# A hybrid encoder layer on one core: side tasks cut into steps at each change of engine, and residual pieces emitted one a k tile

## The chip, the cores and the metric

The kernel runs on one NeuronCore of a Trainium2 chip. The metric is the device time of one execution in microseconds (us); lower is better. The core has a matrix engine (PE, with its weight loads shown apart as PEld), three engines for everything else (DVE, ACT and POOL), and a queue for transfers (SP). Each engine works through its own instructions strictly in the order in which the program emitted them, and waits on semaphores for what others produce.

## What is computed

One layer of an encoder on 256 tokens of width 2048, in float32:

```
h = rmsnorm(x);  q,k,v (8 heads x 128), u (512), q_mem (4 heads x 128) = h @ w_in
y_na  = neighbourhood attention over the 256 tokens, learned bias per head
y_ssm = S5 state space mixer: increments, a scan in both directions, output, GELU, GLU
y_mem = cross attention of q_mem into 256 memory tokens (w_mem_kv)
x = x + rmsnorm(concat(rmsnorm(y_na), rmsnorm(y_ssm), rmsnorm(y_mem)) @ w_out)
x = x + rmsnorm(square(relu(rmsnorm(x) @ w_ff1)) @ w_ff2)
```

## The kernel before

All weights come as one stream of chunks of 128 x 1024 floats, in the order in which PE uses them. Each chunk is loaded (`wraw`, three buffers), rounded on ACT to a high part (`wh`) and subtracted on DVE to a low part (`wl`), so that each product of float32 is made of three (in the MLP of two wider) PE products. `take()` hands the next tile of weights to the main stream, and at each new chunk first emits the conversion of the chunk two ahead. So a conversion that stands late in ACT's or DVE's queue holds up PE two chunks later.

Between the main products stand side tasks, written as Python generators: attention heads (`att_task`: scores, softmax `P`, transposes `PT`, output), preparation of the state space matrices (`prep_b`, `prep_c`, `k0`), its increments (`incr`), its scan (`tree`, products `ps` and sums `XS` on DVE alone), its output (`ssm_out`), and the splits of results into high and low parts. `tick()`, called twice a chunk, lets tasks take steps up to their next `yield`. Nothing of this runs on the chip: it fixes the order in which each engine's instructions are emitted.

The order is set by a planner. It keeps a clock for each engine (`clk["V"]` for DVE, `"A"` for ACT, `"G"` for POOL, `"E"` for PE), and every instruction books a cost on its engine's clock (a DVE product of n elements, for one, 72 + 1.04 n ns). Within one step `chain` carries the end of one engine's work into the start of the next one's; a new step starts with an empty chain. After a plain `yield` the task's next step may be taken when PE's clock has passed the chain's end plus `MARGIN` (200 ns), for attention tasks 1200 ns more; after `yield True` it may be taken at once, as long as the engine's clock is not ahead of PE's by more than a bound (2600 ns on DVE, 3000 on ACT, 1700 for the scan). A plain `yield` behind a series of `yield True` has booked nothing in its own step, so the step behind it may be taken at the next tick.

The second edit stands at the head of the MLP. There the residual x1 = x + normed output of the mixer is made in column pieces (`x1_part`): ACT (for the last 512 columns DVE) scales the piece of `acc1`, POOL adds it to `x1`, each twice, once for 128 tokens. `h_prep(k)` transposes columns 128 k on of `x1` on PE and splits them into `hs`. The first MLP product runs over k tiles of 128 rows, with six outputs each, and emits `h_prep(k + 2)` ahead of tile k. Columns 0 to 512 are made ahead of the loop, the rest in six pieces of 256 columns inside it; piece j is transposed first by the `h_prep` that stands ahead of k tile 2 j + 2.

Of the kernel before, what the change touches and what calls it, by code (L numbers as in the profile page):

```python
# [102 lines left out]
def hybrid_kernel(ctx: ExitStack, tc: tile.TileContext, A: dict, out: bass.AP, dbg=None):  # L103
# [81 lines left out]
    def act(o, i, f=AF.Copy, **kw):  # L185
        ACT.activation(o, i, f, **kw)

    def split(h, l, src, g):

        act(h, src, AF.Copy, scale=g)  # L190
        stt(l, src, g, h.bitcast(F32), mult, sub)
# [79 lines left out]

    def wait_for(g):
        while live(g):
            yield


# [379 lines left out]
    def prep_b(ut):  # L656
        yield from until(lambda: ut in loaded and clk["E"] > loaded[ut][1])
        raw = loaded[ut][0]
        w = a2.tile([128, 2, 2, 4, 4, 16], F32, name="W", tag="W", bufs=1)
        par = a2.tile([128, 4, 2, 2, 4], F32, name="par", tag="par", bufs=1)  # L660
        for i, x in enumerate((cfr, cfi, lbr, lbi)):
            act(par[:, i], x[:, 8 * ut:8 * ut + 8].rearrange("p (d q) -> p d q", d=2)[:, :, None, :]
                .to_broadcast([128, 2, 2, 4]))
        for l in range(4):
            o = w[:, :, :, :, l, :]
            src = (w[:, :, :, :, l - 1, :].rearrange("p d c q b -> p (d c q) b") if l
                   else raw.rearrange("p (n b) -> p n b", b=16))
            r_, i_ = (par[:, 2 * min(l, 1) + i].rearrange("p d c q -> p (d c q)")[:, :, None].to_broadcast([128, 16, 16])
                      for i in range(2))
            t = a2.tile([128, 2, 2, 4, 16], F32, name="pt", tag="pt", bufs=1)  # L670
            tt(V, t.rearrange("p d c q b -> p (d c q) b"), src, i_, mult)
            tt(V, o.rearrange("p d c q b -> p (d c q) b"), src, r_, mult)
            tt(V, o[:, :, 0], o[:, :, 0], t[:, :, 1], sub)
            tt(V, o[:, :, 1], o[:, :, 1], t[:, :, 0], add)
            yield True
        yield
        act(W0[ut].rearrange("p d c q j b -> p (d c q) j b"),
            w[:, :, :, :, 0, :].rearrange("p d c q b -> p (d c q) b")[:, :, None, :].to_broadcast([128, 16, 2, 16]))
        w0_done.add(ut)
        if ut % 2 == 0:  # L680
            XS[ut // 2] = a2.tile([128, 2, 16, NB], F32, name="XS", tag="AB", bufs=2)
        for d in range(2):
            for j in range(2):
                h = slice(64 * j, 64 * j + 64)
                act(wx[h, :, ::-1 if d == 0 else 1, j, :], w[h, d].rearrange("p c q l b -> p (c q) l b"))
            yield
            wt = a2.tile([128, 2, 4, 128], F32, name="W1T", tag="W1T", bufs=2)
            for c in range(2):
                p = att()
                for q in range(4):  # L690
                    PE.transpose(p[:, q * 128:(q + 1) * 128], wx[:, 4 * c + q].rearrange("p l j b -> p (l j b)"), ident)
                act(wt[:, c].rearrange("p q m -> p (q m)"), p)
            spawn(incr(ut, d, wt, clk["A"] + MARGIN), 2, "A")
            yield
        yield from until(lambda: (ut, 1) in xs_part)
# [20 lines left out]
    def prep_c(ut):  # L716
        cw = a2.tile([128, 4, 2, 8, 16], F32, name="Cw", tag="ps" if ut < 2 else "W", bufs=1)
        nc.sync.dma_start(cw[:, 0], A["c"][:, ut])
        yield from after(6000.0)
        act(cw[:, 0, 1], cw[:, 0, 1], AF.Copy, scale=-1.0)  # L720
        for l in range(1, 4):
            C, L = cw[:, l - 1], cw[:, l]
            t = a2.tile([128, 2, 8, 16], F32, name="pt", tag="pt", bufs=1)
            tt(V, t, C, bcd(lbi, ut, 1, 16), mult)
            tt(V, L, C, bcd(lbr, ut, 1, 16), mult)
            tt(V, L[:, 0], L[:, 0], t[:, 1], add)
            tt(V, L[:, 1], L[:, 1], t[:, 0], sub)
            yield True
        yield
        for j in range(2):  # L730
            h = slice(64 * j, 64 * j + 64)
            act(CCs[ut % 2][h, :, 16 * j:16 * j + 16], cw[h].rearrange("p l c q b -> p (l c q) b"))
        CC[ut] = CCs[ut % 2].rearrange("p (l c q) b -> p l c q b", l=4, c=2)
        yield
# [21 lines left out]
    def tree(g):  # L756

        X = XS[g]
        cols = slice(16 * g, 16 * g + 16)
        for up, l in [(1, l) for l in range(LEV)] + [(0, l) for l in range(LEV - 2, -1, -1)]:  # L760
            h = 1 << l
            d0 = 2 * h - 1 if up else 3 * h - 1
            n = len(range(d0, NB, 2 * h))
            dst, src = X[:, :, :, d0::2 * h], X[:, :, :, d0 - h:NB - h:2 * h]
            t = a2.tile([128, 2, 16, NB // 2], F32, name="ps", tag="ps", bufs=1)[:, :, :, 0:n]
            tt(V, t, src[:, ::-1], pw[:, l, 0:2, cols][:, :, :, None].to_broadcast([128, 2, 16, n]), mult)
            yield True
            tt(V, dst, dst, t, add)
            yield True
            tt(V, t, src, pw[:, l, 2, cols][:, None, :, None].to_broadcast([128, 2, 16, n]), mult)  # L770
            yield True
            tt(V, dst, dst, t, add)
            yield True
        yield

    yg = uT
    yHL = {}
# [1 line left out]
    def ssm_out(ut):  # L779
        p = att()  # L780
        BD = BD2[:, ut % 2]
        for n, (m, i, k, o) in enumerate(((0, 0, 3, 0), (3, 1, 3, 1), (1, 0, 2, 1), (4, 2, 2, 1), (2, 0, 1, 2),
                                          (5, 3, 1, 1))):
            PE.matmul(p[:, o * NB:(o + k) * NB], BD[:, m, :], uT[:, ut, i * NB:(i + k) * NB], start=(n == 0),
                      stop=False, skip_group_check=True)
        H = XS[ut // 2]
        for i in range(4):
            for d in range(2):
                l = (i + 1) % 4 if d == 0 else (4 - i) % 4
                for c in range(2):  # L790
                    for q in range(4):
                        h = H[:, c, 8 * (ut % 2) + 4 * d + q, :]

                        if d == 0:
                            o0, h = (1, h[:, 0:NB - 1]) if l else (0, h)
                        else:
                            o0, h = (0, h[:, NB - 2::-1]) if l else (0, h[:, ::-1])
                        n = NB - 1 if l else NB
                        PE.matmul(p[32 * q:32 * q + 32, i * NB + o0:i * NB + o0 + n], CC[ut][:, l, c, 4 * d + q, :],
                                  h, start=False, stop=(i == 3 and d == 1 and c == 1), skip_group_check=True,  # L800
                                  tile_position=(0, 32 * q))

        y = yg[:, ut, :]
        t = a2.tile([128, 256], F32, name="gt", tag="gt", bufs=1)
        stt(y, y, col(V_D, ut), p[:, 0:256], mult, add)
        act(t, y, AF.Square)
        out_done.add(ut)
        yield
        ts(t, t, 0.044715, mult, 1.0, add, eng=G)
        tt(G, t, t, y, mult)  # L810
        act(t, t, AF.Tanh, scale=math.sqrt(2.0 / math.pi))
        yield
        stt(yg[:, ut, :], t, 1.0, y, add, mult)
        if dbg:
            dbg(f"y{ut}", y)
        yield
# [42 lines left out]
    def ssm_fin():  # L859
        yHL["H"] = a2.tile([128, 4, 256], F32R, name="yH", tag="AB", bufs=2)  # L860
        yHL["L"] = a2.tile([128, 4, 256], F32R, name="yL", tag="AB", bufs=2)
        half = const.tile([128, 1], F32, name="half")
        V.memset(half, 0.5)
        for ut in range(4):
            split(yHL["H"][:, ut, :], yHL["L"][:, ut, :], yg[:, ut, :], half)
            yield True


    def att_task(qk, vt, bias, hl, name, gcol):
# [15 lines left out]
            act(P[:, t, :], P[:, t, :], AF.Exp, bias=mn[:, t:t + 1], scale=-1.0, accum_out=sm[:, t:t + 1])  # L885
        yield
        V.reciprocal(sm, sm)
        for t in range(2):
            act(P[:, t, :], P[:, t, :], AF.Copy, scale=sm[:, t:t + 1])
        yield  # L890
# [12 lines left out]
        if gcol is None:  # L903
            act(hl, p[:, 0:256])
        else:
            split(hl[0], hl[1], p[:, 0:256], gcol)
        sumsq(name, p[:, 0:256])
        yield


    for ut in range(2):
# [142 lines left out]
    def na_fin():  # L1054
        for h in range(NAH):
            yield from wait_for(naT[h])
            split(mixn[:, 0, h, :], mixn[:, 1, h, :], yna[:, h, :], col(V_NA, h))
            yield

    def na_rms():  # L1060
        yield from wait_for(nf)
# [206 lines left out]
    for k in range(KT):  # L1268
# [12 lines left out]
                PE.matmul(pg[o][:, 256:512], w[1 - i], hs[:, k, i, :], start=False, stop=False, skip_group_check=True)  # L1281
        if k == 0:
            h_prep(2)
        if k % 2 == 0 and k < 12:
            x1_part(slice(128 * k + 512, 128 * k + 768))
    A1.close()
    C = ExitStack()
    cp = C.enter_context(tc.tile_pool(name="cp", bufs=1, side="left"))
# [203 lines left out]
```

## Time and profile before

| | |
|---|---|
| median of 3 runs | 1166.17 us (1164.01 to 1166.64) |
| the profiled execution | 1163.6 us, its span 1161.8 us, mean granted PE clock 0.992 |
| PE busy | 1127.8 us, 97% of the span |
| DVE, ACT, POOL busy | 718.3, 586.0, 94.7 us |
| HBM | 182 GB/s over the span |

The rows further down come from the profiled execution. Times in them are us from the start of the span; an engine's row has start, length, engine, line (L154 is the helper that records every operation, so rows are told apart by their tiles), operation, output <- inputs, and in brackets the idle time of the engine ahead of it with what ended it.

### The profile page before, as it was taken

Reading aid. Unit: us, or ns where it says so; the run is one execution under the profiler, and the core shown is the slowest. Engines: PE = TensorE matmul, PEld = TensorE weight load, DVE = VectorE, ACT = ScalarE, POOL = GpSimd, SP = SyncE. Lnnn points to the kernel's source line nnn. Section 1 sums busy time; section 2 is a strip of 40 time slices with the busy share of each in tenths; the row PEclk is TensorE's granted clock in tenths of the full one; section 3 lists DMA queues with packets and bytes.
Section 4 is the critical chain, followed back from the end, with each engine's and each line's share of the span. In section 5 each row is a group of like instructions: output and inputs, shape, how many; then the busy total and the mean of one; then the engine's idle time right before and its main releaser. Section 6 shows DMA issues by size and latency. Waiting matters only on the chain.

```text
span 1161.8 us, 17423 instructions
## 1 busy us (share of the span) xinstructions
PE 1127.8 (97%) x6776; PEld 972.8 (84%) x6776; DVE 718.3 (62%) x1066; ACT 586.0 (50%) x908; POOL 94.7 (8%) x163
## 2 busy tenths in 40 slices
PE   8999998899999998999999999999999999999996
PEld 8988898789878877888888888888888888888885
DVE  7778477887875675776665444445666665454454
ACT  6586755635663565554455434434444444344341
POOL 1850000000000043000000000000000000011000
PEclk9999999999999999999999999999999999999999
DMA  8874453344444675556666666566666666666663
GB/s 317 291 237 148 149 168 104 106 142 150 138 153 126 205 233 172 176 187 187 193 192 188 184 190 189 181 197 185 195 185 194 187 188 192 186 197 195 190 210 128
DMA packets 62723, 213.05 MB, mean 183 GB/s; under 512 B 7216, under 2 KB 8752, under 8 KB 62640
## 3 DMA queue, kind: packets, MB, share of 16 engines
q1 hardware_dynamic: 62352, 211.84, 58.1%
q8 instruction: 53, 0.87, 0.3%
q14 instruction: 30, 0.25, 0.1%
q10 hardware_dynamic: 288, 0.09, 0.0%
HBM read 209.81 MB, written 2.10 MB: 182 GB/s over the span
## 4 chain that ended last, share of the span: by engine, by line
PE 78%; DVE 6%; ACT 5%; POOL 4%; DMA 3%; issue 3%; SPq 0%; DVEq 0%; ACTq 0%; POOLq 0%
PE acc L154 70%; PE att L154 4%; DMA wraw<-in_w_dram 3%; PE big L154 3%; DVE wl L154 3%; ACT wh L154 3%; POOL x L154 1%; DVE XS L154 1%; ACT P L154 1%; POOL u L154 1%; DVE ps L154 1%; POOL acc L154 0%; ACT wx L154 0%; POOL t L154 0%; POOL q L154 0%
## 5 line engine op out<-in xcount | busy, mean ns | idle before, releaser
L154 DVE TENSOR_TENSOR wl<-wraw,wh 128x1024 fp32r<-128x1024 f32 (+1 forms) x372 | 455.3, 1226 | 383.8 <-ACT wh L154 383.2
L154 ACT ACTIVATE wh<-wraw 128x1024 fp32r<-128x1024 f32 (+1 forms) x372 | 391.2, 1053 | 418.4 <-PE acc L154 340.4
L154 PE MATMUL acc<-hs,wh 128*128 128x512 f32 (+1 forms) x996 | 345.9, 391 | 0.0
L154 PE MATMUL acc<-hs,wl 128*128 128x256 f32 x992 | 279.3, 282 | 0.0
L154 PEld LDWEIGHTS acc<-hs,wh 128*128 128x128 f32 x996 | 186.8, 188 | 38.8 <-ACT hs L154 0.2
L154 PEld LDWEIGHTS acc<-hs,wl 128*128 128x128 f32 x992 | 187.3, 189 | 0.0
L154 PE MATMUL acc<-wh,fH 128*128 128x512 f32 x448 | 178.7, 399 | 0.0
L154 PE MATMUL acc<-wh,fL 128*128 128x512 f32 x448 | 176.5, 394 | 0.0
L154 PE MATMUL acc<-wl,fH 128*128 128x512 f32 x448 | 175.7, 392 | 0.0
L154 PEld LDWEIGHTS acc<-wh,fL 128*128 128x128 f32 x448 | 84.1, 188 | 22.0
L154 PEld LDWEIGHTS acc<-wl,fH 128*128 128x128 f32 x448 | 84.1, 188 | 19.8
L154 PEld LDWEIGHTS acc<-wh,fH 128*128 128x128 f32 x448 | 84.1, 188 | 19.4
L154 PE MATMUL acc<-xH,wh 128*128 128x256 f32 x256 | 75.6, 295 | 0.0
L154 PE MATMUL acc<-xH,wl 128*128 128x256 f32 x256 | 72.4, 283 | 0.0
L154 PE MATMUL acc<-xL,wh 128*128 128x256 f32 x256 | 72.4, 283 | 0.0
L154 PEld LDWEIGHTS acc<-xH,wh 128*128 128x128 f32 x256 | 48.9, 191 | 0.8
L154 PEld LDWEIGHTS acc<-xL,wh 128*128 128x128 f32 x256 | 48.9, 191 | 0.4
L154 PEld LDWEIGHTS acc<-xH,wl 128*128 128x128 f32 x256 | 48.8, 191 | 0.0
L154 POOL TENSOR_TENSOR facc<-facc,g 128x512 f32<-128x512 f32 x6 | 9.0, 1528 | 475.1 <-DMA g<-in_g_dram 475.1
L154 PE MATMUL acc<-wh,mixn 128*128 128x512 f32 x128 | 42.1, 404 | 0.0
L154 DVE TENSOR_TENSOR ps<-XS,pw 128x32 f32<-128x32 f32 (+9 forms) x44 | 30.8, 700 | 1.1
L154 DVE TENSOR_TENSOR XS<-XS,ps 128x32 f32<-128x32 f32 (+9 forms) x44 | 29.4, 668 | 0.8
(304 smaller groups left out, 1486.2 us busy)
## 6 DMA issues: line engine op xcount, KB each, us to landing
wraw<-in_w_dram SPq DMA_DIRECT2D x369, 512.0 KB, 4.3
tokst<-in_xt_dram SPq DMA_DIRECT2D x4, 512.0 KB, 6.8
mst<-in_memT_dram SPq DMA_DIRECT2D x4, 512.0 KB, 5.1
tokst<-in_mt_dram SPq DMA_DIRECT2D x4, 512.0 KB, 5.8
bias<-in_bias_dram SPq DMA_DIRECT2D x8, 256.0 KB, 4.0
x<-in_xt_dram SPq DMA_DIRECT2D x8, 256.0 KB, 5.1
out_dram<-facc SPq DMA_DIRECT2D x8, 256.0 KB, 2.5
xst<-in_xT_dram SPq DMA_DIRECT2D x7, 256.0 KB, 5.8
```

Source lines behind the costliest of these rows:

```text
L154: return f(o, *a, **kw)
```

## The change

Two edits. The first: a step of a side task now ends where its work goes from one engine to another. Where there was a plain `yield` (or nothing) behind a series on ACT or DVE, `done(e)` lets the task go on only when PE's clock has passed that engine's booked end plus 200 ns. `split_task` puts a step's end between the high part on ACT and the low part on DVE; `att_task` gets one behind the reciprocal and one ahead of the low part of a memory head; `ssm_out` gets two. The second: the residual pieces are emitted behind k tiles 0 to 5 and not behind 0, 2, 4, ... 10. Instructions, sizes and buffers stay the same.

```diff
+    def split_task(h, l, src, g):
+        act(h, src, AF.Copy, scale=g)
+        yield
+        stt(l, src, g, h.bitcast(F32), mult, sub)
...
+    def done(e):
+
+        t = clk[e] + MARGIN
+        while clk["E"] < t:
             yield
...
@@ prep_b
                 .to_broadcast([128, 2, 2, 4]))
+        yield from done("A")
...
             yield True
-        yield
+        yield from done("V")
...
@@ prep_c
         act(cw[:, 0, 1], cw[:, 0, 1], AF.Copy, scale=-1.0)
+        yield from done("A")
...
             yield True
-        yield
+        yield from done("V")
...
@@ tree
             tt(V, dst, dst, t, add)
             yield True
-        yield
+        yield from done("V")
...
@@ ssm_out
         stt(y, y, col(V_D, ut), p[:, 0:256], mult, add)
+        out_done.add(ut)
+        yield
         act(t, y, AF.Square)
-        out_done.add(ut)
         yield
         ts(t, t, 0.044715, mult, 1.0, add, eng=G)
         tt(G, t, t, y, mult)
+        yield
         act(t, t, AF.Tanh, scale=math.sqrt(2.0 / math.pi))
...
@@ att_task
         V.reciprocal(sm, sm)
+        yield
         for t in range(2):
             act(P[:, t, :], P[:, t, :], AF.Copy, scale=sm[:, t:t + 1])
...
-            split(hl[0], hl[1], p[:, 0:256], gcol)
+            act(hl[0], p[:, 0:256], AF.Copy, scale=gcol)
         sumsq(name, p[:, 0:256])
         yield
+        if gcol is not None:
+            stt(hl[1], p[:, 0:256], gcol, hl[0].bitcast(F32), mult, sub)
+            yield
...
@@ na_fin
-            split(mixn[:, 0, h, :], mixn[:, 1, h, :], yna[:, h, :], col(V_NA, h))
-            yield
+            yield from split_task(mixn[:, 0, h, :], mixn[:, 1, h, :], yna[:, h, :], col(V_NA, h))
...
@@ the MLP's first product
-        if k % 2 == 0 and k < 12:
-            x1_part(slice(128 * k + 512, 128 * k + 768))
+        if k < 6:
+            x1_part(slice(256 * k + 512, 256 * k + 768))
```

What this does to the engines' orders shows at three places.

The end of the second scan on DVE, before. `ps` and `XS` of 32x31 are the scan's last level; `ssm_out` on PE, which reads `XS`, stands in PE's order among the products of the output projection (`mixn`), 12 main products behind the place where the projection's head results begin.

```order
L154 TENSOR_TENSOR wl<-wraw,wh 128x1024
L154 TENSOR_TENSOR ps<-XS,pw 128x32x31
L154 TENSOR_TENSOR XS<-XS,ps 128x32x31
L154 SCALAR_TENSOR_TENSOR mixn<-yna,vecs,mixn 128x256 x3
L154 TENSOR_TENSOR ps<-XS,pw 128x32x31
L154 SCALAR_TENSOR_TENSOR mixn<-yna,vecs,mixn 128x256
L154 TENSOR_TENSOR wl<-wraw,wh 128x1024
L154 TENSOR_TENSOR XS<-XS,ps 128x32x31
```

The same end in the changed kernel. It now stands ten conversions earlier, between those of the last head's weights (conversions are counted in DVE's order), and `ssm_out` stands among the products of the last head, 120 main products earlier in PE's order.

```order
L154 TENSOR_TENSOR wl<-wraw,wh 128x1024
L154 SCALAR_TENSOR_TENSOR P<-att,bias 128x512
L154 TENSOR_REDUCE mn<-P 128x2
L154 TENSOR_TENSOR XS<-XS,ps 128x32x31
L154 TENSOR_TENSOR wl<-wraw,wh 128x1024
L154 TENSOR_TENSOR ps<-XS,pw 128x32x31
L154 TENSOR_TENSOR XS<-XS,ps 128x32x31
```

The densest place of the changed kernel on ACT, in the stretch of the first four heads. `W1T` goes to an increment's products on PE, `PT` to a head's output, `wx` and `P` to transposes.

```order
L154 ACTIVATE wh<-wraw 128x1024
L154 ACTIVATE PT<-att 128x512
L154 ACTIVATE P<-P,sm 128x256 x2
L154 ACTIVATE XS<-att 128x2x256
L154 ACTIVATE wx<-W 64x32x16 x2
L154 ACTIVATE mixm<-att,vecs 128x256
L154 ACTIVATE sq<-att 128x256
L154 ACTIVATE PT<-att 128x512
L154 ACTIVATE P,sm<-P,mn 128x256 x2
L154 ACTIVATE W1T<-att 128x512 x2
L154 ACTIVATE wh<-wraw 128x1024
```

Here the work of three tasks that stood spread over some five conversions in the kernel before stands between two of them.

The MLP's head on ACT, before: `acc` is a residual piece scaled (two halves), `hs` the high part of a k tile.

```order
L154 ACTIVATE hs<-att,vecs 128x256
L154 ACTIVATE acc_3744<-acc_3744,r_4594 128x256 x2
L154 ACTIVATE hs<-att,vecs 128x256
L154 ACTIVATE wh<-wraw 128x1024
L154 ACTIVATE hs<-att,vecs 128x256
L154 ACTIVATE wh<-wraw 128x1024
L154 ACTIVATE acc_3744<-acc_3744,r_4594 128x256 x2
L154 ACTIVATE hs<-att,vecs 128x256 x2
L154 ACTIVATE wh<-wraw 128x1024
L154 ACTIVATE acc_3744<-acc_3744,r_4594 128x256 x2
L154 ACTIVATE hs<-att,vecs 128x256
L154 ACTIVATE wh<-wraw 128x1024
```

And in the changed kernel: the piece for the next pair of k tiles stands one k tile earlier, and the one behind it two, three ahead; from the fifth piece on they are DVE's.

```order
L154 ACTIVATE hs<-att,vecs 128x256
L154 ACTIVATE acc_3822<-acc_3822,r_4594 128x256 x2
L154 ACTIVATE hs<-att,vecs 128x256
L154 ACTIVATE wh<-wraw 128x1024
L154 ACTIVATE acc_3822<-acc_3822,r_4594 128x256 x2
L154 ACTIVATE hs<-att,vecs 128x256
L154 ACTIVATE wh<-wraw 128x1024
L154 ACTIVATE acc_3822<-acc_3822,r_4594 128x256 x2
L154 ACTIVATE hs<-att,vecs 128x256
L154 ACTIVATE acc_3822<-acc_3822,r_4594 128x256 x2
L154 ACTIVATE hs<-att,vecs 128x256
L154 ACTIVATE wh<-wraw 128x1024
```

## Rows read from the trace of the kernel before

**Rows 1.** The page's part 1: busy time, share of the span and instructions of each engine.

```profile
PE 1127.8 (97%) x6776; PEld 972.8 (84%) x6776; DVE 718.3 (62%) x1066; ACT 586.0 (50%) x908; POOL 94.7 (8%) x163
```

**Rows 2.** Busy time of each engine in three stretches: the side tasks, the MLP's head, and the MLP. Columns: stretch, its length, busy us (and instructions) of PE, PEld, DVE, ACT and POOL, granted PE clock, DMA share, GB/s.

```profile
120.00:360.00 240.00, 225.95 (x1964) 204.19 (x1966) 177.65 (x300) 138.89 (x265) 12.54 (x16) 0.97 0.44 137
420.00:480.00 60.00, 55.41 (x332) 47.50 (x331) 35.73 (x56) 32.91 (x59) 20.09 (x19) 1.00 0.54 171
480.00:1120.00 640.00, 640.00 (x3211) 540.65 (x3210) 357.08 (x435) 291.44 (x388) 9.75 (x7) 1.00 0.62 190
```

**Rows 3.** The same view in the four stretches of the side tasks in which the granted clock is at half.

```profile
191.60:195.00 3.40, 3.40 (x18) 3.40 (x18) 2.18 (x5) 1.01 (x5) 0.00 (x0) 0.50 0.40 108
229.10:232.50 3.40, 3.40 (x14) 3.01 (x13) 3.33 (x5) 1.19 (x3) 0.72 (x1) 0.51 0.55 154
314.50:317.90 3.40, 3.40 (x10) 2.67 (x11) 3.37 (x4) 2.19 (x4) 0.00 (x0) 0.50 0.44 161
348.60:352.00 3.40, 3.40 (x76) 2.95 (x65) 0.55 (x2) 0.42 (x1) 0.54 (x2) 0.50 0.71 233
```

**Rows 4.** PE in order of time, the places of the side tasks at which it was idle for over 0.8 us.

```profile
130.80 0.43 PE L154 MATMUL att<-U,W1T 128*128 128x64 f32 x2 [0.83 <-ACT W1T L154]
189.89 0.32 PE L154 MATMUL att<-U,W1T 128*128 128x64 f32 x1 [3.18 <-ACT W1T L154]
213.78 0.45 PE L154 MATMUL att<-PT,v 128*128 128x256 f32 x1 [1.55 <-DVE qk L154]
228.00 1.22 PE L154 MATMUL att<-U,W1T 128*128 128x64 f32 x9 [0.88 <-ACT W1T L154]
266.96 0.91 PE L154 MATMUL att<-CC,W 128*32 128x96 f32 x32 [1.60 <-ACT CC L154]
314.41 0.88 PE L154 MATMUL att<-ident,P 128*128 128x128 f32 x2 [2.52 <-ACT P L154]
347.59 1.67 PE L154 MATMUL att<-XS,CC 128*32 128x63 f32 x88 [2.52 <-DVE XS L154]
```

**Rows 5.** ACT and DVE in order of time, just ahead of the last three of these places.

```profile
264.79 2.12 ACT L154 ACTIVATE CC<-Cw 64x1024 f32<-64x1024 f32 x2 [2.66 <-DVE Cw L154]
313.85 0.91 ACT L154 ACTIVATE P<-P,sm 128x256 f32<-128x256 f32 x2 [3.22 <-DVE sm L154]
339.65 1.73 DVE L154 TENSOR_TENSOR ps<-XS,pw 128x992 f32<-128x992 f32 x1
346.35 1.18 DVE L154 TENSOR_TENSOR XS<-XS,ps 128x992 f32<-128x992 f32 x1
```

**Rows 6.** PE in order of time, the transposes of `x1` that stand ahead of k tiles of the first MLP product.

```profile
438.38 0.38 PE L154 MATMUL att<-ident,x 128*128 128x128 f32 x2
440.74 0.33 PE L154 MATMUL att<-ident,x 128*128 128x128 f32 x1
443.67 0.38 PE L154 MATMUL att<-ident,x 128*128 128x128 f32 x2
445.99 0.38 PE L154 MATMUL att<-ident,x 128*128 128x128 f32 x2
457.56 0.33 PE L154 MATMUL att<-ident,x 128*128 128x128 f32 x1 [1.37 <-POOL x L154]
465.88 0.38 PE L154 MATMUL att<-ident,x 128*128 128x128 f32 x2
```

**Rows 7.** POOL, ACT and DVE in order of time in the same stretch: two of the pieces' sums on POOL, the scaling of the later of them on ACT, the weights' subtraction beside it, and a later subtraction with no sum beside it.

```profile
431.14 1.43 POOL L154 TENSOR_TENSOR x<-x,acc 128x256 f32<-128x256 f32 x2 [3.13 <-ACT acc L154]
439.31 2.06 POOL L154 TENSOR_TENSOR x<-x,acc 128x256 f32<-128x256 f32 x2 [3.23 <-ACT acc L154]
438.74 0.90 ACT L154 ACTIVATE acc<-acc,r 128x256 f32<-128x256 f32 x2
438.87 1.22 DVE L154 TENSOR_TENSOR wl<-wraw,wh 128x1024 fp32r<-128x1024 f32 x1 [1.30 <-ACT wh L154]
453.17 1.23 DVE L154 TENSOR_TENSOR wl<-wraw,wh 128x1024 fp32r<-128x1024 f32 x1 [0.46 <-ACT wh L154]
```

**Rows 8.** ACT and DVE in order of time, operations of the dense place (the pair of exponentials with its sums runs from 180.32 to the conversion at 181.31).

```profile
180.32 0.50 ACT L154 ACTIVATE P<-P,mn 128x256 f32<-128x256 f32 x1
181.31 1.05 ACT L154 ACTIVATE wh<-wraw 128x1024 fp32r<-128x1024 f32 x1
189.26 1.07 ACT L154 ACTIVATE W1T<-att 128x512 f32<-128x512 f32 x2
178.73 0.68 DVE L154 SCALAR_TENSOR_TENSOR P<-att,bias 128x512 f32<-128x512 f32 x1
179.45 0.69 DVE L154 TENSOR_REDUCE mn<-P 128x2 f32<-128x512 f32 x1
```

**Rows 9.** PE in order of time, products of the dense place (two of the main products, twelve apart, and two whole side groups), and the first products of `ssm_out`.

```profile
302.48 0.28 PE L154 MATMUL acc<-xH,wh 128*128 128x256 f32 x1
303.90 0.28 PE L154 MATMUL acc<-xH,wh 128*128 128x256 f32 x1
343.42 1.65 PE L154 MATMUL att<-uT,BD 128*128 128x192 f32 x12
183.39 1.02 PE L154 MATMUL att<-PT,v 128*128 128x256 f32 x4
184.25 1.04 PE L154 MATMUL att<-ident,wx 128*128 128x128 f32 x8
```

More of the change, by code (lines that the diff above doesn't have):

```diff
@@ L864, in ssm_fin @@
         for ut in range(4):
-            split(yHL["H"][:, ut, :], yHL["L"][:, ut, :], yg[:, ut, :], half)
-            yield True
+            yield from split_task(yHL["H"][:, ut, :], yHL["L"][:, ut, :], yg[:, ut, :], half)
     def att_task(qk, vt, bias, hl, name, gcol):
@@ L905, in att_task @@
         else:
-            split(hl[0], hl[1], p[:, 0:256], gcol)
+            act(hl[0], p[:, 0:256], AF.Copy, scale=gcol)
         sumsq(name, p[:, 0:256])
         yield
+        if gcol is not None:
+            stt(hl[1], p[:, 0:256], gcol, hl[0].bitcast(F32), mult, sub)
+            yield
     for ut in range(2):
```

## The prediction

> **What bounds the kernel now.** I read the page's busy times first. PE is busy 97% of the span, every other engine 62% or less [rows 1], so a microsecond is won only where PE waits or runs slowly. Next I cut the span into stretches. From 480 to 1120 us PE is busy all 640 us: nothing in the MLP's bulk can be won, and whatever PE gains ahead of it moves the end by as much. From 120 to 360 us, the side tasks, PE is busy 225.95 of 240 us, 14.0 idle; from 420 to 480 us, the MLP's head, 55.41 of 60, 4.6 idle [rows 2]. The 14.0 are no lack of throughput: in that stretch DVE is busy 177.65 us, 74%, and ACT 138.89, 58%.
>
> Then I asked who ends those waits. Seven places hold 13.1 of the 14.0 us: three times PE stands at an increment's product and waits for `W1T` from ACT (0.83, 3.18, 0.88), once for a bank that `qk` on DVE frees (1.55), once for `CC` from ACT (1.60), once for `P` from ACT (2.52), once for the scan's `XS` from DVE (2.52) [rows 4]. Just ahead of them stand the engines that were late, and they too had been idle: ACT for 2.66 us at the head of its queue until DVE gave `Cw`, 3.22 until DVE gave a sum's reciprocal; the scan's last sum began at 346.35 and PE had been waiting for it since 345.1 [rows 4, 5]. An instruction that is emitted before what it needs is done blocks all that stands behind it on its engine, conversions of weights among it.
>
> Each long wait has a second price. In four stretches of 3.4 us the granted clock is 0.50 or 0.51, the 1.2 GHz level, and each of the four begins just behind one of these waits [rows 3, 4]. At half clock PE does 1.7 us of work in 3.4, so the four cost 6.8 us.
>
> **The change part by part.** No instruction is added or taken away, so the busy sums stay; only order moves.
>
> The residual pieces. A clean k tile takes 2.32 us, from one pair of transposes to the next (443.67 to 445.99). From 438.38 to 465.88 PE runs ten k tiles in 27.50 us, against 23.2, so 4.3 us are lost, at waits for `x` from POOL [rows 6]. The cause is distance: the sums of piece 1 start at 439.31 behind a scaling that ACT began at 438.74, take 2.06 us, and PE wants the piece from 440.74 on [rows 6, 7]. In the new order that scaling stands one k tile earlier, 2.3 us; the later pieces are ahead by 4.6 us and more. None of the waits seen (1.37 us the longest in the rows) is as long as that. Supply holds: a piece takes POOL 2.06 us and a k tile lasts 2.32. Piece 0 doesn't move and its wait, ahead of 438.38, stays. So −4.3 us. Its bounds: 0, if the POOL is late all the same, and 4.6, all idle time of the stretch.
>
> On that supply the Trainium skill speaks against the change. Its page "SBUF — State Buffer", section "Who interferes with whom", says that a DVE instruction with two SBUF inputs and a GpSimd instruction that reads SBUF shut each other out, the later one waiting until the first is done. The trace agrees by half: two sums took 1.43 us alone and 2.06 where they began at 439.31, inside a subtraction that ran from 438.87 to 440.09, and the 0.63 more is nearly what that had left; the subtraction took 1.22 us, one with no sum beside it 1.23 [rows 7]. A subtraction held up by a sum no row here shows. With sums at 2.06 the term is −4.3; by the rule's other half it would be as the third rival below prices it.
>
> The side tasks' steps. With `done`, ACT's `CC` and `W0` copies are emitted only when DVE is booked as finished, `P` only behind its reciprocal, and `ssm_out` only behind the scan's end. The order shows it: the second scan ends ten conversions earlier, and `ssm_out` no longer stands among the output projection's products. So I take all seven waits as removed with their clock falls: −14.0 − 6.8 = −20.8 us.
>
> What is late next is the price of it. First, the dense places. Tasks that waited now come together, at three places between the first head and the last of the memory heads, and I replayed the densest by hand. PE comes to the second increment's product behind `qk`, eight transposes (1.04 us), twelve main products (1.42) and a head's output (1.02), 3.5 us in all [rows 9]. What that product needs starts at the same `qk`: DVE's scores and minimum (0.68 and 0.69), then ACT's two exponentials (0.99) and, behind them in its queue, `W1T` (1.07): 3.4 us [rows 8]. Every handover between engines comes on top, so PE waits there, a little. The nearest rows are the two short waits for `W1T`, 0.83 and 0.88; the trace's worst wait of the kind costs 3.18 + 1.7 us [rows 3, 4]. I take 0.9 at each of three places, +2.7 us, since the two chains are of nearly one length. Bounds: 0, and 3 × 4.9 = 14.7.
>
> Second, the scan's end. The planner books 72 + 1.04 × 992 ns, 1.10 us, for an operation on the scan's last level; the rows have 1.73 for `ps` and 1.18 for `XS` [rows 5]. Two of each end 2 × 0.63 + 2 × 0.08 = 1.4 us later than booked; 200 ns margin and the products that `ssm_out` does before it reads `XS`, up to 1.65 us [rows 9], hide that nearly to nothing. I take +0.5; bounds 0 and the present 2.52 + 1.7 = 4.2.
>
> The other edits cost nothing that I can find: splits in two steps leave 0.4 us of DVE work for a later tick, and every consumer of them (`mixn`, `yH`) is read a chunk or more later on PE. Weight transfers keep their place in SP's queue, behind the same conversions; small loads for the state space stand earlier in it, and wait for products that PE now does earlier too.
>
> The sum: −4.3 − 14.0 − 6.8 + 2.7 + 0.5 = −21.9 us. Against the profiled execution's own 1163.6 that is 1141.7. That execution lies 2.6 us under the median of the three runs, so for a median of the new kernel I add half of that: **1143 us**. A change of 0.2%, 2.3 us, is about what the runs' own spread (1164.0 to 1166.6) lets one tell from none.
>
> **The rivals.**
> - *The dense places pay in full.* The three places go as the worst wait of before did, 4.9 us each, 14.7 in all in place of 2.7. For it: all three engines have their work there in one lump, and ACT holds ten operations between two conversions. Against it: the chains worked out above are of one length with PE's own work. Time: 1143 + 12 = 1155. Chance 0.15.
> - *Only the pieces gain.* The waits of the side tasks move and don't shrink, because tasks that step later have less time left until the products that need them. Against it: in the order the last of them comes earlier. Time: 1143 + 17.6 = 1161. Chance 0.08, 0.03 of it inside the 0.2%.
> - *Sums and subtractions shut each other out.* If POOL's sums (1.43 us a piece alone) and the weights' subtraction cannot overlap, each of five k tiles with a new piece delays the subtraction by up to one sum, 0.72 us, and so PE: 3.6 us come back. Time: 1146.6. Chance 0.08; the rule of the skill named above is this one.
> - *Late by a little everywhere*, the way to a slower kernel. Some 40 side groups on PE now stand 200 ns behind the booked end of what they need. If bookings run short in general, as 1.10 against 1.73 us does, PE waits at each. The gain of 25.1 is used up, and 2.3 more, at a mean of 27.4 / 40 = 0.69 us; at 1.0 us each the time is 1165 − 25.1 + 40 = 1180. Against it: in the trace of before, with the same bookings, all waits outside the seven places come to 14.0 − 13.1 = 0.9 us. Chance 0.05.
> - *More than forecast.* Ends of products are modelled, so part of each wait is hidden in a busy PE; no new waits and some such part (0.2 to 0.3 us at some twenty places) would give 1143 − 3.2 − 5 = 1135 or less. Chance 0.04 for under 1134.
>
> **How the numbers follow.** The forecast, with its neighbourhood of 1134 to 1150, has 0.60. The range of 1134 to 1157 adds the third rival and most of the first: 0.60 + 0.08 + 0.13 = 0.81. Faster by over 0.2%: 0.60 + 0.15 + 0.05 + 0.08 + 0.04 = 0.92. Within: 0.03. Slower: 0.05.
>
> **What would show it.** Right: PE idle from 120 to 340 us under 5 us, at most one stretch at half clock there, transposes of `x1` at even 2.32 us from the fourth k tile on, and the MLP's bulk still at 100%. Wrong: waits of over 2 us for `W1T` or for a bank near the first four heads' end (first rival); waits for `x` left on PE (third); many waits of 0.5 to 1 us for ACT and DVE spread over all side groups (fourth).

## The result and the profile after

The changed kernel takes 1150.36 us (median; 1149.33 to 1151.43) beside 1165.99 us for the kernel before, run along with it. The ratio is 0.9869, with a 95% interval of 0.9852 to 0.9886: 15.3 us faster, between 13.3 and 17.3. The profiled execution took 1149.86 us, its span is 1148.1 us, its mean granted clock 0.996. Against the profiled execution of before, 1163.6 us, that is 13.7 us; the forecast for the same difference was 21.9. The time lies inside the range, 7 us above the number.

The page's part 1 of the changed kernel, which answers to [rows 1]:

```profile
PE 1120.9 (98%) x6776; PEld 968.7 (84%) x6776; DVE 719.5 (63%) x1066; ACT 585.9 (51%) x908; POOL 102.0 (9%) x163
```

No engine has more instructions. DVE and ACT are busy as long as before, to within 1.2 us; POOL is busy 7.3 us longer with the same 163 instructions.

The stretches of [rows 2] in the changed kernel, set so that they hold about the same products (the side tasks end 8.95 us earlier, at 351.05; the MLP begins about 9 us earlier), and the one stretch at half clock that is left. Columns as in [rows 2].

```profile
121.00:351.05 230.05, 220.69 (x2002) 200.78 (x2001) 177.49 (x292) 139.87 (x269) 19.34 (x18) 0.99 0.45 139
411.00:471.00 60.00, 58.48 (x357) 51.43 (x356) 39.98 (x63) 35.28 (x63) 20.72 (x19) 1.00 0.59 185
471.00:1111.00 640.00, 640.00 (x3204) 540.30 (x3204) 355.75 (x429) 290.37 (x386) 9.67 (x7) 1.00 0.62 191
282.60:286.00 3.40, 3.38 (x12) 3.02 (x13) 3.33 (x6) 1.74 (x3) 0.00 (x0) 0.51 0.91 311
```

PE's idle time among the side tasks fell from 14.0 us to 230.05 − 220.69 = 9.4, where under 5 was forecast; in the MLP's head from 4.6 to 1.5. Four stretches at half clock became one. The MLP's bulk is still busy all of its 640 us.

PE in order of time, the places of the side tasks where it was idle for over 0.4 us, which answers to [rows 4]:

```profile
160.41 0.92 PE L154 MATMUL att<-qk 128*128 128x256 f32 x3 [1.12 <-DVE qk L154]
180.31 0.88 PE L154 MATMUL att<-U,W1T 128*128 128x64 f32 x6 [1.30 <-ACT W1T L154]
198.39 1.13 PE L154 MATMUL att<-qk 128*128 128x256 f32 x4 [1.67 <-DVE qk L154]
213.42 1.10 PE L154 MATMUL att<-qk 128*128 128x256 f32 x4 [0.46 <-ACT wh L154]
222.26 1.09 PE L154 MATMUL att<-ident,wx 128*128 128x128 f32 x8 [2.30 <-ACT wx L154]
282.62 2.08 PE L154 MATMUL att<-qk 128*128 128x256 f32 x4 [1.96 <-DVE qk L154]
```

The waits of before for `CC`, `P` and (but for 0.4 us) `XS` are gone, those for `W1T` are down to one. In their place stand six waits of 8.8 us in all. Four of them are at a head's scores, and three of these wait for `qk`, which DVE makes from the head's projection; [rows 4] has no wait of PE's at scores.

ACT shows where they come from. Groups of its instructions over the side tasks, of the kernel before (105 to 350 us); columns: tiles, shapes and count, then busy us and mean ns, then the idle time ahead of them and what ended it:

```profile
L154 ACT ACTIVATE P<-P,mn 128x256 f32<-128x256 f32 x24 | 12.0, 502 | 29.2 <-DVE mn L154 29.2
L154 ACT ACTIVATE P<-P,sm 128x256 f32<-128x256 f32 x24 | 10.9, 501 | 21.9 <-DVE sm L154 21.9
L154 ACT ACTIVATE CC<-Cw 64x1024 f32<-64x1024 f32 x6 | 6.3, 1057 | 2.7 <-DVE Cw L154 2.7
```

And of the changed kernel (105 to 345 us):

```profile
L154 ACT ACTIVATE P<-P,mn 128x256 f32<-128x256 f32 x24 | 12.0, 502 | 47.2 <-DVE mn L154 47.2
L154 ACT ACTIVATE P<-P,sm 128x256 f32<-128x256 f32 x24 | 10.8, 497 | 1.3 <-DVE sm L154 1.3
L154 ACT ACTIVATE CC<-Cw 64x1024 f32<-64x1024 f32 x6 | 6.3, 1057 | 2.2 <-DVE Cw L154 2.1
```

ACT's standing at the head of its queue did not go, it moved. With the changed order 20.6 us of waiting for `sm` are gone, and the waiting for `mn` has grown by 18.0. `mn` is the minimum of the scores on DVE, and the exponentials that read it are emitted in the same step as the scores: this is the one handover from DVE to ACT in the attention tasks that the change left inside a step. Behind these exponentials stand conversions of weights, `W1T` and `wx`.

Four of these exponentials on ACT, in order of time:

```profile
153.92 0.51 ACT L154 ACTIVATE P<-P,mn 128x256 f32<-128x256 f32 x1 [4.57 <-DVE mn L154]
178.68 0.51 ACT L154 ACTIVATE P<-P,mn 128x256 f32<-128x256 f32 x1 [2.85 <-DVE mn L154]
187.34 0.51 ACT L154 ACTIVATE P<-P,mn 128x256 f32<-128x256 f32 x1 [3.98 <-DVE mn L154]
219.46 0.51 ACT L154 ACTIVATE P<-P,mn 128x256 f32<-128x256 f32 x1 [4.98 <-DVE mn L154]
```

The last wait of the list above followed back on ACT and DVE:

```profile
274.35 0.51 ACT L154 ACTIVATE P<-P,mn 128x256 f32<-128x256 f32 x1 [5.18 <-DVE mn L154]
275.35 1.99 ACT L154 ACTIVATE wh<-wraw 128x1024 fp32r<-128x1024 f32 x2
276.43 1.23 DVE L154 TENSOR_TENSOR wl<-wraw,wh 128x1024 fp32r<-128x1024 f32 x1 [2.11 <-ACT wh L154]
280.22 1.22 DVE L154 TENSOR_TENSOR wl<-wraw,wh 128x1024 fp32r<-128x1024 f32 x1
281.88 0.69 DVE L154 TENSOR_TENSOR qk<-acc,rb_x 128x512 f32<-128x512 f32 x1
```

At 274.35 ACT has waited 5.18 us for the minimum; the high parts come behind it; DVE, whose next instruction is the low part, stands idle for 2.11 us with a run of rotations (`pt`, `Cw`) behind it, has no idle time from there on, and reaches `qk` at 281.88, when PE has been waiting since 280.66. The waits for `qk` at 160.41 and 198.39 have the same chain behind the exponentials at 153.92 and 187.34, and DVE stands idle at the low part for 2.11 and 2.20 us. The waits at 180.31 and 222.26 are shorter chains: `W1T` and `wx` themselves stand in ACT's queue behind the exponentials at 178.68 and 219.46.

### The profile page after: what moved, and what is told of

It reads as the page before. It is cut to its first block, busy times and chain, and to the rows that moved or that the text cites. A ratio compares the mean times of both kernels' runs of the same rounds, so it can differ in the third digit from the quotient of the medians.

```text
span 1148.1 us, 17416 instructions
## 1 busy us (share of the span) xinstructions
PE 1120.9 (98%) x6776; PEld 968.7 (84%) x6776; DVE 719.5 (63%) x1066; ACT 585.9 (51%) x908; POOL 102.0 (9%) x163
## 4 chain that ended last, share of the span: by engine, by line
PE 86%; DVE 4%; ACT 4%; DMA 3%; issue 1%; POOL 1%; SPq 0%; DVEq 0%; POOLq 0%; ACTq 0%
PE acc L154 75%; PE att L154 6%; PE big L154 5%; DMA wraw<-in_w_dram 3%; DVE wl L154 2%; ACT wh L154 2%; ACT U L154 1%; POOL acc L154 0%; DMA gpost<-in_post_dram 0%; DVE W L154 0%; ACT P L154 0%; DVE XS L154 0%; POOL x L154 0%; DVE ps L154 0%; ACT tokst L154 0%
## 5 line engine op out<-in xcount | busy, mean ns | idle before, releaser
L154 ACT ACTIVATE P<-P,mn 128x256 f32<-128x256 f32 x24 | 12.0, 502 | 47.2 <-DVE mn L154 47.2
```

The lines of the kernel that those rows point to most:

```text
L154: return f(o, *a, **kw)
```

## The experiments

**Each edit alone.** The pieces alone (the second edit, nothing of the first):

```diff
-        if k % 2 == 0 and k < 12:
-            x1_part(slice(128 * k + 512, 128 * k + 768))
+        if k < 6:
+            x1_part(slice(256 * k + 512, 256 * k + 768))
```

> The kernel before with only the residual pieces emitted one a k tile. My theory: the pieces are worth the 4.3 us that k tiles lost at waits for x, whatever the side tasks do, so about 1161.7 us. Rival, the sums on POOL and the subtractions on DVE shut each other out and 3.6 us come back: about 1165.3 us. In the trace, PE's transposes of x1 at even 2.32 us from the fourth k tile on under the first, waits for x of 0.3 us and more under the second.

Measured: 1161.49 us beside 1164.6, ratio 0.9973 (0.9959 to 0.9987), so 3.1 us, between 1.5 and 4.8. The trace of it, POOL's sums and PE's transposes at the place of [rows 6]:

```profile
437.74 3.47 POOL L154 TENSOR_TENSOR x<-x,acc 128x256 f32<-128x256 f32 x4 [0.85 <-ACT acc L154]
445.75 2.66 POOL L154 TENSOR_TENSOR x<-x,acc 128x256 f32<-128x256 f32 x2 [0.36 <-DVE acc L154]
436.82 0.38 PE L154 MATMUL att<-ident,x 128*128 128x128 f32 x2
439.14 0.38 PE L154 MATMUL att<-ident,x 128*128 128x128 f32 x2
460.02 0.38 PE L154 MATMUL att<-ident,x 128*128 128x128 f32 x2
```

From 436.82 to 460.02 ten k tiles take 23.20 us, 2.32 each; the 27.50 of before are gone, although a piece's two sums take POOL up to 2.66 us where they meet DVE's work (1.43 alone in [rows 7]). Call the PE products that take `wh` or `wl` the main products; their order is the same in all these kernels. Between two of them in the MLP's head (the 2,041st and the 2,341st, before 63.77 us apart) the kernel is 3.92 us shorter, the changed kernel 4.28.

The steps alone: the diff above turned round in the changed kernel.

> The changed kernel with the residual pieces put back behind k tiles 0, 2, ... 10: the steps of the side tasks alone. If the two edits do not touch each other: 1150.4 + 4.3 = 1154.7 us, some 11 us under the kernel before. If the earlier arrival at the MLP or another state of the queues changes what the pieces are worth: up to 1157 or down to 1152.

Measured: 1154.89 us, ratio 0.9922 (0.9903 to 0.9942), 9.1 us faster than before. The two sum to 3.1 + 9.1 = 12.2, against 15.3 for both; each of the three has an interval of some 2 us to each side, so these runs show no part that needs both edits.

**The exponentials.** One more step's end in the changed kernel, in `att_task`:

```diff
         V.tensor_reduce(mn, P, axis=AX.X, op=ALU.min)
+        yield
         for t in range(2):
             act(P[:, t, :], P[:, t, :], AF.Exp, bias=mn[:, t:t + 1], scale=-1.0, accum_out=sm[:, t:t + 1])
```

> The changed kernel with one more step's end, in the attention tasks between the minimum on DVE and the exponentials on ACT. Theory A: the five long waits that are left on PE (1.12, 1.30, 1.67, 2.30 and 1.96 us, and 1.7 us at half clock) all come from exponentials that stand at the head of ACT's queue for 2.9 to 5.2 us until DVE gives the minimum, with conversions and W1T or wx behind them. Then most of 8.4 + 1.7 us goes: 1141 to 1145 us, and no idle of over 1.5 us ahead of an exponential on ACT. Theory B, DVE's queue is filled too far ahead of PE by the rotations of the matrices, and qk stands behind them: then 1149 to 1152 us, and the three waits for qk stay. Theory C, heads that step later run out of time before what needs them: 1152 to 1156 us.

Measured: 1138.35 us (1137.57 to 1141.11), ratio 0.9782 (0.9761 to 0.9803): 25.4 us faster than before, and 10.1 by the ratios, 12.0 by the medians, faster than the changed kernel. The side tasks of this kernel, in the view of the stretches:

```profile
121.00:339.00 218.00, 217.10 (x1999) 199.03 (x1999) 178.80 (x294) 140.20 (x269) 16.74 (x18) 1.00 0.47 146
```

And its group of the exponentials on ACT (105 to 335 us):

```profile
L154 ACT ACTIVATE P<-P,mn 128x256 f32<-128x256 f32 x24 | 11.9, 500 | 3.2 <-DVE mn L154 3.2
```

Waiting for `mn` falls from 47.2 us to 3.2, PE's idle time from 9.4 to 0.9, no stretch of the side tasks is at half clock, and all six waits are gone. Theory A holds, though the time came out below its 1141 to 1145 us, and one exponential still waits 1.8 us, against its sign of at most 1.5. Idle time falls by 8.5 us and half clock gives back 1.7, 10.2 in all; from the 701st to the 1,873rd main product, which spans the side tasks, the trace is 11.4 us shorter than that of the changed kernel. Where the other 1.2 us come from is not shown; part of the waits can have been hidden in a PE that counts as busy.

**DVE filled less far ahead.** The bound of the preparations halved in the changed kernel:

```diff
-BACK_V, BACK_G, BACK_A, BACK_TREE = 2600.0, 4000.0, 3000.0, 1700.0
+BACK_V, BACK_G, BACK_A, BACK_TREE = 1300.0, 4000.0, 3000.0, 1700.0
```

> The changed kernel with the bound by which DVE's booked clock may be ahead of PE's halved for the preparation of matrices, 1300 ns in place of 2600. Theory B (DVE filled too far ahead, qk stands behind rotations): the three waits for qk, 4.75 us, and the stretch at half clock, 1.7 us, go: about 1144 us. Theory A (exponentials at the head of ACT's queue): DVE's backlog comes from its wait for the high parts, which stays, so 1149 to 1153 us; preparations that finish later may cost a little.

Measured: 1157.2 us, ratio 0.994 (0.9919 to 0.9962): slower than the changed kernel by 7 to 8 us, and outside what either theory said. PE in order of time, the three longest waits of this kernel:

```profile
212.78 1.45 PE L154 MATMUL att<-U,W1T 128*128 128x64 f32 x8 [1.76 <-ACT W1T L154]
336.65 0.79 PE L154 MATMUL acc<-wl,mixn 128*128 128x512 f32 x1 [2.36 <-DVE wl L154]
369.82 0.38 PE L154 MATMUL acc<-yH,wh 128*128 128x256 f32 x1 [3.87 <-ACT yH L154]
```

So theory B is half right: the waits for `qk` are gone, and a run of rotations ahead of `qk` is needed for them. But the rotations then come late, the last of them at 346.5 us and not at 279.8, beside the output projection's work, and the state space output `yH` is late for the product that reads it; that the one brings the other is argued from the order, not shown by a run. Behind these three waits the granted clock is 0.50 for 17.0 us in all, where the changed kernel has 3.4. ACT still waits 30.6 us for `mn`. The waits for `qk` could be taken away without loss at the exponentials, and not by this bound.

**Halves of the first edit.** With the pieces in, first only the waits for booked ends (`done`), then only the added ends of steps:

```diff
# only done: in the two preparations and the scan
-        yield
+        yield from done("V")
```

> The pieces, and of the side tasks' steps only the waits for booked ends (done, in the two preparations and the scan). By the waits of before that these can reach (CC 1.60 us; XS 2.52 us with its 1.7 us at half clock): 1161 - 5.8 = about 1155 us, with the waits behind softmax's P (2.52 and 3.18 us) still there. If it is these waits that bring everything, as the earlier end of the second scan suggests: 1150 us. If they alone only defer work: 1161 us or more.

Measured: 1155.56 us (1151.01 to 1157.16), ratio 0.9927 (0.9902 to 0.9951).

```diff
# only ends of steps: the changed kernel without done
-        yield from done("V")
+        yield
```

> The pieces, and of the side tasks' steps only the added ends of steps (behind the reciprocal, between the high and the low parts, in the scan's output), without the waits for booked ends. By the waits of before that these can reach (P 2.52 and W1T behind P 3.18 us, each with 1.7 us at half clock): 1161 - 9.1 = about 1152 us, with the waits for CC and XS, or what takes their place, still there. If the two halves need each other: 1156 to 1161 us.

Measured: 1149.22 us (1147.45 to 1153.59), ratio 0.9878 (0.9856 to 0.9901), the same as the whole change. The first half met its 1155 us, but by luck: the waits for `CC` and `XS` are gone, and so are those of 2.52 us for `P` and 3.18 for `W1T`, which it was not to reach, with new ones for `qk` and `W1T` in their place (2.15, 1.95 and 1.86 us the longest). In the second half (its profiled execution took 1153.59 us, the longest of the six) the waits for `CC` and `XS` are gone as well, although `done` is not there, and the longest new one is 2.83 us for `W1T`. So `done` is not needed for those two waits to go. Beside the pieces alone the first half is worth 5.4 us by the ratios, the second 11.1, both 12.1, each good to some 3 us: what `done` adds to the second half lies within the noise. The waits of these kernels belong to the order as a whole, not to single edits. ACT waits 29.5 us for `mn` in the first half and 41.0 in the second.

**The step's end alone.** The kernel before with the pieces and the one added line ahead of the exponentials, without anything of the first edit.

> The kernel before with the pieces and one added step's end alone, that between the minimum on DVE and the exponentials on ACT; nothing else of the change. Theory A says that this handover blocks ACT whatever the others do, and in the changed kernel it was worth 12 us: about 1149 to 1153 us here. If it is worth so much only where the other handovers have been cut (ACT then waits at P or CC in its place): 1156 to 1162 us.

Measured: 1140.8 us (1139.02 to 1141.7), ratio 0.9801 (0.9778 to 0.9825), below the 1149 to 1153 of theory A. ACT waits 1.2 us for `mn`; PE is idle for 1.8 us among the side tasks (216.20 of 218.00 busy), and no stretch of them is at half clock. One line does 20 us where the whole first edit did 9 to 12, and the first edit adds little to it: 0.9801 against 0.9782, intervals that overlap.

The scaling by `sm`, which this kernel leaves uncut, on ACT (105 to 345 us):

```profile
L154 ACT ACTIVATE P<-P,sm 128x256 f32<-128x256 f32 x24 | 10.8, 501 | 26.7 <-DVE sm L154 26.7
```

ACT waits there even longer than before (26.7 us against 21.9, 5.05 the longest), and PE hardly notices. So ACT's waiting in us is not by itself a price: that at `sm` cost little once that at `mn` was gone. Why the one holds PE up and the other does not, no run here shows.

**The distance behind the minimum.** The line with 200 ns behind the booked end in place of 1400:

```diff
         V.tensor_reduce(mn, P, axis=AX.X, op=ALU.min)
-        yield
+        yield True
+        yield from done("V")
```

> The changed kernel with the end of a step ahead of the exponentials, as in the run that gave 1138 us, but with 200 ns behind the booked end of the minimum in place of 1400. If the longer distance is what keeps ACT from waiting: waits for the minimum on ACT come back in part, 1139 to 1146 us. If 200 ns do and heads gain time: 1136 to 1138.5 us.

Measured: 1138.95 us, ratio 0.9782 (0.9758 to 0.9805), the same time; ACT waits 2.6 us ahead of these exponentials, so the bookings are good enough for 200 ns. The version that beats both kernels is the changed one with the added line, at either distance.

## Why the prediction was right, and where it was off

**The sign and the place** were right: the gain is in the two stretches that were named, and the MLP's bulk follows unchanged. Of the signs named ahead, the even transposes and the single stretch at half clock came; idle time under 5 us did not. That the time lies inside the range is owed to the room that the range left for the first rival's price; of the forecast 21.9 us, 8.2 are missing.

**The pieces, −4.3.** 4.28 us in the trace of the changed kernel. A piece does not come late any more from the fourth k tile on. The distance was worked out rightly; supply was tighter than the 2.06 us a piece of the prediction, since two sums took up to 2.66 us beside DVE's work, more than a k tile, and the lead of the later pieces covered it. With the edit alone the runs give 3.1, between 1.5 and 4.8.

**The lock-out rival** was refused for its price, rightly, but on a wrong reading. The prediction says that no row shows a subtraction held up by a sum. The trace of before has one, in the MLP's bulk; POOL's two sums, the subtraction on DVE, and its twin without a sum:

```profile
1022.58 3.29 POOL L154 TENSOR_TENSOR facc<-facc,g 128x512 f32<-128x512 f32 x2 [391.21 <-DMA g<-in_g_dram]
1025.04 1.91 DVE L154 TENSOR_TENSOR wl<-wraw,wh 128x1024 fp32r<-128x1024 f32 x1 [1.57 <-ACT wh L154]
1027.79 1.23 DVE L154 TENSOR_TENSOR wl<-wraw,wh 128x1024 fp32r<-128x1024 f32 x1 [0.84 <-ACT wh L154]
```

The second of these sums of `facc` ran from 1024.58 to 1025.87, and the subtraction that came at 1025.04 ended at 1026.95, 1.08 us behind that sum's end: nearly its whole 1.23 us lie behind it. It cost no time, because DVE has slack there: PE is busy all the while. The rule of the Trainium skill, page "SBUF — State Buffer", section "Who interferes with whom", that whichever of the two comes second waits for the first to end, agrees with this row and with [rows 7], one for each order: the later one took 0.68 us longer where 0.83 of the sum were left, and 0.63 longer where 0.78 of the subtraction were left.

**The seven waits, −20.8.** The named waits went (of the last, 0.4 us stayed), and so did their four stretches at half clock. The sum took off all 14.0 us of idle time, 0.9 more than the seven waits held. The reason given for three of them is not borne out: the prediction has `done` take away the waits for `CC` and `XS` and the step's end behind the reciprocal that for `P`, but each half of the edit alone took away all three.

**What is late next, +2.7 and +0.5: the step that failed.** The scan's end was sized well (0.4 us of waiting for `XS` against 0.5). The other term was mis-sized: new waits cost 8.8 us and one stretch at half clock, 1.7, so 10.5 in place of 2.7. In the trace the stretch from the 701st to the 1,873rd main product is 10.2 us shorter than before, where −20.8 + 2.7 + 0.5 = −17.6 was forecast: 7.4 of the 8.2 us between forecast and result. Most of the rest lies ahead of the side tasks, where the changed kernel's execution is 1.2 us late at the 701st main product (that of the pieces alone, whose order is that of before up to the MLP, is 1.1 late). The error was one of kind, not of numbers alone. The prediction looked for new waits at three dense places and priced them by two chains of equal length, minimum, exponentials, `W1T`. It had the row of the exponentials [rows 8] and took their duration from it, but did not ask what ACT did ahead of them: in the same trace ACT stood 29.2 us at exponentials, more than at `sm` (21.9) and `Cw` (2.7) together, and the change leaves that handover uncut. It followed back only waits that end at PE's longest gaps. The group of the exponentials would have said that the largest wait of ACT stays; and in the changed kernel the queue, which no longer stops at `sm`, stands at `mn` for 18.0 us more.

**The booking of the scan.** The 1.73 us for `ps` against 1.10 booked was a disturbed row. The other product of that size in the same scan of the kernel before, and one in the changed kernel that met a sum on POOL from 222.98 to 223.72:

```profile
343.71 1.18 DVE L154 TENSOR_TENSOR ps<-XS,pw 128x992 f32<-128x992 f32 x1
223.15 1.61 DVE L154 TENSOR_TENSOR ps<-XS,pw 128x992 f32<-128x992 f32 x1
```

In [rows 5] the product began at 339.65 inside a sum on POOL that lasted from 338.91 to 340.34. So the booking is short by 0.1 us, not 0.6, and the term was right at 0.5 by luck, for a reason that was not there.

**The rivals.** ACT's waiting moved and hardly shrank, which comes near the second (the three groups shown above sum to 53.8 us before and 50.7 after), but not because tasks ran out of time: with one more step's end they were faster. The price was some two thirds of the first rival's, spread over six waits and not three places. "Late by a little everywhere" did not show: behind six waits, all others come to 0.6 us.

## What to carry to other kernels

When an in-order engine is late, list the idle time ahead of each group of its instructions, not only the wait that ends at the bound engine: leaving aside work that waits for the bound engine itself, the group with the largest sum is the first handover to try a cut at. Here one step's end at that group was worth 20 us, and the cuts elsewhere about half of that, with the queue's waiting moved to the uncut handover. The sum says where to try, not what it is worth: 26.7 us of waiting at another handover cost little. A bound on how far work runs ahead was no substitute here: it freed the waits for `qk`, and work that it held back came late.

## What the runs showed of the hardware

**Clock falls do not follow from a wait alone.** In the changed kernel the clock fell to the 1.2 GHz level at 282.6, behind a wait of 1.96 us, and stayed at 2.4 GHz behind one of 2.30 us at 219.97. In the kernel with the pieces alone the wait of 0.88 us for `W1T` that had a fall behind it in [rows 3, 4] comes again, and so does that for `XS`, 2.41 us where it was 2.52, and neither has a fall behind it:

```profile
229.19 0.99 PE L154 MATMUL att<-U,W1T 128*128 128x64 f32 x7 [0.88 <-ACT W1T L154]
347.21 0.98 PE L154 MATMUL att<-XS,CC 128*32 128x63 f32 x56 [2.41 <-DVE XS L154]
```

The stretches behind them, in the view of the stretches, at a granted clock of 1.00:

```profile
229.00:232.40 3.40, 3.21 (x22) 2.99 (x23) 3.37 (x5) 0.99 (x3) 0.00 (x0) 1.00 0.37 80
348.00:351.40 3.40, 3.40 (x100) 3.00 (x89) 0.98 (x4) 0.42 (x1) 1.04 (x2) 1.00 0.79 246
```

That kernel's executions go from 1159.29 us at a mean granted clock of 0.994 to 1163.78 at 0.991, so a part of the spread of a kernel with such waits may come from how many falls an execution has; this is argued, since only one execution of each kernel has a trace. The forecast's 6.8 us for four falls was right for the profiled execution, and is no fixed price of the waits.

**POOL sums and DVE products of two SBUF inputs lengthen each other.** In the rows shown, a DVE product that starts inside a POOL sum is longer by 0.4 to 0.7 us (1.61 against 1.18; 1.91 against 1.23), and a piece's two sums on POOL by 0.6 to 1.2 (2.06 and 2.66 against 1.43). The low parts `hs`, with one input in SBUF and one in PSUM, took 0.48 us inside the POOL sums of 439.31 to 441.37 as they did with no sum beside them:

```profile
440.02 0.48 DVE L154 SCALAR_TENSOR_TENSOR hs<-att,vecs,hs 128x256 fp32r<-128x256 f32 x1
452.22 0.48 DVE L154 SCALAR_TENSOR_TENSOR hs<-att,vecs,hs 128x256 fp32r<-128x256 f32 x1 [1.79 <-ACT hs L154]
```

POOL's 7.3 us of longer busy time in the changed kernel can come from more such meetings; no run here took them away.
